# Two ordinary weight tiles per Strassen tile in a SwiGLU FFN, with the ordinary groups in three PSUM banks and the gated outputs held as one fp32 copy

## The chip, the cores and the metric

The kernel runs on one core of one Trainium2 chip. The core has a matrix engine (TensorE, "PE" in the profile, with its weight loads as "PEld"), a vector engine (VectorE, "DVE"), an activation engine (ScalarE, "ACT"), a general engine (GpSimd, "POOL") and a queue that issues the transfers from memory (SyncE, "SP"). Matrix products are collected in eight PSUM banks of 512 fp32 columns. The metric is the device time of one execution in microseconds (us), the median of a few runs. A lower time is better.

## The reference

Two layers work on 256 tokens of width 2048: a recurrent block and then sliding-window attention, each followed by a SwiGLU feed-forward network (FFN). The change concerns the FFN, which appears once in each layer:

```python
D_MODEL = 2048; SEQ = 256; D_FF = 5632

def swiglu_ffn(x, g, w_in, w_out):
    h = rms_norm(x, g)
    gate, up = jnp.split(h @ w_in, 2, axis=-1)
    return x + (jax.nn.silu(gate) * up) @ w_out
```

Everything is fp32. All weights are read once, so every product has 256 columns (the tokens) on one side.

## The kernel before

Weights arrive as tiles of 128 partitions x 1024 fp32 values (512 KB). A *tile* is one job of the list `self.jobs`. The loop `stream` (L309) takes the jobs in order: at job i it issues the load of job i+4 on SP's queue (`load`, L236), splits the weights of job i+3 (`split`, L281), and then emits the matmuls of job i. There are four buffers each for `raw`, `hi` and `lo`. A split makes from an fp32 tile a rounded high part (ACT, L295, or L287 for Strassen tiles) and the rest, the low part (DVE, L298, or L288). A product of two fp32 matrices is then three matmuls: high x high, high x low, low x high.

An **ordinary tile** (`group`, L378, and `products`, L327, whose matmuls are line L361) has two blocks of 128 input features (k) and four of 128 output features (f): 2 x 4 x 3 = 24 matmuls of 256 columns. Eight tiles make one *group* with four outputs of 128 x 256 (two gates and two ups). A group keeps its sums in PSUM banks in one of three ways. By default it takes four banks; where `sync` is given, two of its outputs then have the high x high product and the high x low product in two halves of one bank, and such a pair of matmuls can be issued as one of 512 columns ("h" in `PARTS`). With `paired` it takes two banks with two outputs in each and has no 512 wide matmuls. With `packed` it takes three: two outputs with a bank each, which can have 512 wide matmuls, and two outputs together in the third. The 512 wide matmuls come in runs of three, in the tiles that `sync` names (0, 2 and 5 of eight) and after a matmul of another kind (`pe_other`, L365, which sets `self.runs`).

A **Strassen tile** (`strassen`, L432, matmuls on L460) needs seven block products where an ordinary one has eight, so 21 matmuls. In exchange POOL adds and subtracts blocks of the weights (`sums`, L267, lines L277 to L279), and both ACT and DVE split three pieces: 768 columns of the tile and twice 512 columns of sums. The other side's sums (`form`, L477, POOL lines L488 to L491) are made once per FFN. A Strassen group is eight tiles too and takes four banks. The first `NS` = 4 groups of an FFN's first product are Strassen groups, the other 18 are ordinary.

`ffn` (L637) builds two lists, `turns` (32 Strassen tiles) and `ordinary` (144 tiles), and puts four ordinary tiles (`AHEAD`) first, then one Strassen tile and one ordinary tile in turn until the Strassen tiles are used up, and then the rest. Here this mixed stretch is called the Strassen stage. In it ordinary groups 4 to 8 are `paired`, so that 4 + 2 x 2 banks hold a Strassen group and two ordinary groups. The later ordinary groups take four banks with `sync`.

When an ordinary group ends, `done` (L687) pulls its four outputs out of PSUM (`pull`, L502: for an output with one half in use, a product with `rstd` on DVE; for one with two halves, a copy on ACT and an add on DVE ahead of it), and a background task applies SiLU (ACT), multiplies gate by up (DVE) and splits the result into a high and a low part (`split_act`, L520) which take one slot of 128 x 512 for each 128 x 256 output. When a Strassen group ends, `fast` (L643) combines the four banks with one ACT copy and four DVE adds into `U` and `V`; a task applies SiLU and the product (L134 on DVE), waits four ticks (`yield 4`; a tile has two ticks), has PE transpose the results (L369 and L372), and splits them from PSUM. Background tasks are issued when the planner's account of ACT and DVE time has room (`run_bg`, L208). Slots (58, `self.slots`) also hold the normalised input, the forms and the sums. The second product of the FFN, `ffn_out`, uses the split outputs `hid` and follows after all the tiles of the first.

Of the kernel before, what the change touches and what calls it, by code (L numbers as in the profile page):

```python
# [12 lines left out]
F32 = mybir.dt.float32  # L13
F32R = mybir.dt.float32r
AF = mybir.ActivationFunctionType
ALU = mybir.AluOpType
# [3 lines left out]
T = 256  # L20
DFF = 5632
ND = D // P
# [27 lines left out]
class Trunk:  # L50
# [17 lines left out]

    NS = 4
    AHEAD = 4  # L70
    SPACE = 14

    def __init__(self, ctx, tc, dram):
# [355 lines left out]
                    done([(p, two, st["bank"][b] if last_of else None) for p, two, b, last_of in st["ps"]])  # L429
            jobs.append((src(c), mm))  # L430

    def strassen(self, src, xs, forms, done, last):  # L432

        st = {}
        jobs = []
        for c in range(ND // 2):
            part = {}

            def mm(hi, lo, c=c, part=part):
                if c == 0:  # L440
                    st["ps"] = [self.bank() for _ in range(4)]
                    st["begun"] = set()
                ps = st["ps"]
                x2 = [self.need(xs[2 * c + kt]) for kt in range(2)]
                fh, fl = self.need(forms[c])
                A = lambda kt, b: tuple(x2[kt][:, q + b * P:q + b * P + P] for q in (0, T))
                S = lambda n: tuple(q[:, n * P:n * P + P] for q in (fh, fl))
                B = lambda n: tuple(q[:, n * T:n * T + T] for q in (hi, lo))
                s = part["set"]
                t1, t3, t2, t4 = (tuple(s[n + q][:, h * T:h * T + T] for q in (0, 1)) for n in (2, 4) for h in range(2))  # L450
                todo = [(0, 0, A(0, 0), B(1)), (1, 1, A(1, 0), B(3)), (1, 0, S(1), t2), (2, 0, S(0), t1),
                        (2, 1, S(2), t3), (3, 0, S(3), B(2)), (3, 1, A(1, 1), t4)]
                if self.other is not None:
                    self.runs = self.RUNS
                    self.other = None
                for n, (b, h, w, m) in enumerate(todo):
                    if n == 4:
                        self.half_tick()
                    for i, j in ((0, 0), (0, 1), (1, 0)):
                        self.nc.tensor.matmul(ps[b][:, h * T:h * T + T], w[i], m[j], start=b not in st["begun"],  # L460
                                              stop=c == ND // 2 - 1 and i == 1, skip_group_check=True)
                        st["begun"].add(b)
                        self.since += 1
                if last and c == ND // 2 - 1:
                    for q in self.sets:
                        for t in q:
                            self.free(t)
                    self.sets = None
                if last:
                    for q in (fh, fl):  # L470
                        self.free(q)
                if c == ND // 2 - 1:
                    done(ps)
            jobs.append((src(c), mm, part))
        return jobs

    def form(self, c, col, out):  # L477

        while len(self.slots) < self.SPACE:
            yield 1  # L480
# [156 lines left out]
    def ffn(self, l, xs, forms, r, gains, rn, out=None):  # L637
        hid = [Val() for _ in range(NH)]
        w = self.d[f"ffn_in{l}"]
        one = self.con[:, K_ID:K_ID + P]  # L640
        turns, ordinary = [], []
        for g in range(self.NS):
            def fast(ps, g=g):  # L643
                c1, U, V = self.t(), self.slot(F32), self.slot(F32)
                two = lambda q: q.rearrange("p (b t) -> p b t", b=2)
                twice = lambda q: q.unsqueeze(1).broadcast_to([P, 2, T])
                self.a(c1, ps[0][:, 0:T])
                self.tt(two(U[:, :]), two(ps[1][:, :]), twice(c1[:, :]), ALU.add)
                self.tt(two(V[:, :]), two(ps[2][:, :]), twice(U[:, 0:T]), ALU.add)
                self.tt(U[:, 0:T], ps[2][:, 0:T], V[:, T:2 * T], ALU.add)  # L650
                self.tt(V, ps[3], V, ALU.add)
                for b in ps:
                    self.free_bank(b)

                def task():
                    while not self.rv[r].ready:
                        yield 1
                    rs = [self.rstd[r][:, T + b:T + b + 1] for b in range(2)]
                    for q, s in ((U, 0), (V, 1)):
                        self.a(q[:, T:2 * T], q[:, T:2 * T], AF.Silu, scale=rs[s])  # L660
                    yield
                    for q, k, s in ((V, U, 0), (U, V, 1)):
                        self.stt(q[:, 0:T], q[:, 0:T], rs[s], k[:, T:2 * T], ALU.mult, ALU.mult)
                    yield 4
                    while not self.room():
                        yield 1
                    p = self.mbank()
                    for h in range(2):
                        for b, q in enumerate((V, U)):
                            self.pe_other(p[:, h * T + b * P:h * T + b * P + P], q[:, h * P:h * P + P], one,  # L670
                                          f=self.nc.tensor.transpose)
                    yield 1
                    self.free(U)
                    self.free(V)
                    for h in range(2):
                        while not self.slots:
                            yield 1
                        s = self.slot()
                        self.split_act(s, p[:, h * T:h * T + T])
                        hid[2 * g + h].ap = s  # L680
                        hid[2 * g + h].ready = True
                        yield
                    self.free_mbank(p)
                self.spawn(task())
            turns += self.strassen(lambda c, g=g: w[g, c], xs, forms, fast, g == self.NS - 1)
        for g in range(self.NS, NH // 2):
            def done(ps, g=g):  # L687
                rs = self.rstd[r][:, 0:T]
                early = not self.rv[r].ready
                v = [self.pull(p, r=None if early else rs) for p in ps]  # L690

                def task():
                    while not self.rv[r].ready:
                        yield 1
                    for h in range(2):
                        ga, up = v[2 * h], v[2 * h + 1]
                        if early:
                            self.tt(ga, ga, rs, ALU.mult)
                            self.tt(up, up, rs, ALU.mult)
                        self.a(ga, ga, AF.Silu)  # L700
                        yield
                        self.tt(ga, ga, up, ALU.mult)
                        while not self.slots:
                            yield 1
                        s = self.slot()
                        self.split_act(s, ga)
                        self.free_half(ga)
                        self.free_half(up)
                        hid[2 * g + h].ap = s
                        hid[2 * g + h].ready = True  # L710
                        yield
                self.spawn(task())
            self.group(lambda c, g=g: w[g, c], ND, xs, done, g == NH // 2 - 1, self.SYNC,
                       paired=2 * (g <= 2 * self.NS), jobs=ordinary)
        n = len(turns)
        self.jobs += ordinary[:self.AHEAD]
        for q in zip(turns, ordinary[self.AHEAD:]):
            self.jobs += q
        self.jobs += ordinary[self.AHEAD + n:]
        self.project(self.d[f"ffn_out{l}"], NH, hid, gains, rn, out)  # L720


# [610 lines left out]
```

## Time and profile before

| | us |
|---|---|
| median of 3 runs | 2023.13 (2022.03 to 2024.72) |
| the profiled execution | 2023.72 |
| its span, first to last instruction | 2021.9 |
| PE / DVE / ACT / POOL busy in the span | 1985.0 / 1412.9 / 1122.3 / 376.7 |
| mean granted PE clock | 0.995 |
| matmuls recorded | 16699 |

In the profile a line such as L361 is a line of the kernel above, and a group names the tile that is written, an arrow and the tiles that are read: `b` is a PSUM bank, `s` a slot, `raw`, `hi` and `lo` the weight buffers, `h` a 128 x 256 half, `x` the residual stream. "x848 | 115.6, 276 | 0.0" means 848 instructions, 115.6 us busy in total (overlaps counted once), 276 ns mean length of one, and the engine's idle time just before them. Matmuls are pipelined: each is listed with some 276 ns, though one starts about every 113 to 118 ns. The pace of PE is therefore read from starts, not from lengths.

### The profile page before, as it was taken

The page shows a single profiled execution, that of the slowest core. Times are in us where ns is not written, and L with a number is a line of the kernel's source. Part 1 is how long each engine was busy: PE and PEld are TensorE (multiplying, and loading weights), DVE is VectorE, ACT ScalarE, POOL GpSimd, SP SyncE. Part 2 cuts the span into 40 slices and gives each one's busy share as a digit, 9 for nine tenths or more (in the row PEclk, how much of TensorE's full clock was granted, in tenths as well). Part 3 has the DMA queues.
Part 4 walks back from the last instruction along what each step waited for, and adds up shares of the span by engine and source line. Part 5 has one row for each costly group of instructions (what it writes and reads, how often), then busy time and mean ns, then how long its engine had stood idle before and what let it go on. Part 6 is the DMA issues. An engine that isn't in the chain of part 4 may idle for free.

```text
span 2021.9 us, 41009 instructions
## 1 busy us (share of the span) xinstructions
PE 1985.0 (98%) x16699; PEld 1943.6 (96%) x16699; DVE 1412.9 (70%) x2089; ACT 1122.3 (56%) x1754; POOL 376.7 (19%) x356
## 2 busy tenths in 40 slices
PE   9999998999999999999999999989999999999999
PEld 9999998999999999999999889889999999999999
DVE  8988979999655655545667767889866556554553
ACT  6799766555444444434556776555555445444342
POOL 0000136774000000000002453576700000000000
PEclk9999999999999999999999999999999999999999
DMA  8555654555555555555555435455555655556663
GB/s 279 189 182 186 209 173 161 188 180 193 194 198 191 196 192 195 193 194 198 190 190 164 139 123 175 160 173 182 176 192 192 196 195 190 197 197 201 207 209 125
DMA packets 106204, 377.15 MB, mean 187 GB/s; under 512 B 11936, under 2 KB 14368, under 8 KB 106016
## 3 DMA queue, kind: packets, MB, share of 16 engines
q1 hardware_dynamic: 105408, 373.88, 56.0%
q8 instruction: 130, 2.13, 0.4%
q10 hardware_dynamic: 608, 0.66, 0.1%
q14 instruction: 58, 0.48, 0.1%
HBM read 371.88 MB, written 2.10 MB: 185 GB/s over the span
## 4 chain that ended last, share of the span: by engine, by line
PE 83%; DVE 7%; issue 3%; ACT 3%; POOL 2%; DMA 1%; ACTq 0%; DVEq 0%; POOLq 0%; SPq 0%
PE b L361 75%; PE b L460 4%; DVE lo L298 2%; DVE s L288 2%; PE b L372 1%; DVE s L130 1%; ACT hi L295 1%; ACT s L121 1%; DMA raw<-in_ffn_in 1%; DVE lo L288 1%; PE b L826 1%; POOL s L277 1%; PE b L369 1%; POOL s L489 1%; PE b L1012 1%
## 5 line engine op out<-in xcount | busy, mean ns | idle before, releaser
L361 PE MATMUL b<-s,hi 128*128 128x256 f32 (+1 forms) x9474 | 1309.1, 284 | 6.1 <-ACT hi L295 4.9
L361 PEld LDWEIGHTS b<-s,hi 128*128 128x128 f32 x9474 | 1207.5, 189 | 29.0 <-ACT hi L295 5.3
L298 DVE TENSOR_TENSOR lo<-raw,hi 128x1024 fp32r<-128x1024 f32 (+1 forms) x643 | 795.7, 1240 | 501.8 <-ACT hi L295 497.8
L295 ACT ACTIVATE hi<-raw 128x1024 fp32r<-128x1024 f32 (+1 forms) x643 | 675.8, 1054 | 623.4 <-PE b L361 562.1
L361 PE MATMUL b<-s,lo 128*128 128x256 f32 x4992 | 753.1, 277 | 0.0
L361 PEld LDWEIGHTS b<-s,lo 128*128 128x128 f32 x4992 | 655.1, 189 | 0.6
L277 POOL TENSOR_TENSOR s<-raw 128x512 f32<-128x512 f32 x64 | 121.4, 1896 | 115.0 <-DMA raw<-in_ffn_in 98.1
L288 DVE TENSOR_TENSOR s<-s,s 128x512 fp32r<-128x512 f32 x128 | 125.8, 985 | 17.5 <-ACT s L287 17.5
L1102 POOL TENSOR_TENSOR s<-s 128x128 f32<-128x128 f32 x32 | 14.7, 461 | 635.3 <-ACT s L121 630.7
L287 ACT ACTIVATE s<-s 128x512 fp32r<-128x512 f32 x128 | 79.7, 624 | 87.0 <-POOL s L277 48.1
L460 PE MATMUL b<-s,s 128*128 128x256 f32 x768 | 115.4, 283 | 4.4 <-DVE s L288 4.2
L460 PEld LDWEIGHTS b<-s,s 128*128 128x128 f32 x768 | 100.9, 189 | 6.3 <-DVE s L288 6.2
L460 PE MATMUL b<-hi,s 128*128 128x256 f32 x384 | 89.4, 282 | 1.1 <-DVE s L130 0.9
L288 DVE TENSOR_TENSOR lo<-raw,hi 128x768 fp32r<-128x768 f32 x64 | 80.4, 1256 | 0.4
L279 POOL TENSOR_TENSOR s<-raw,s 128x256 f32<-128x256 f32 x64 | 72.5, 1132 | 5.0
L489 POOL TENSOR_TENSOR s<-s 128x128 f32<-128x128 f32 x16 | 16.3, 1017 | 303.4 <-ACT s L121 303.4
L121 ACT ACTIVATE s<-s 128x256 f32<-128x256 f32 (+3 forms) x132 | 51.9, 439 | 37.4 <-POOL s L491 26.4
L460 PEld LDWEIGHTS b<-hi,s 128*128 128x128 f32 x384 | 68.4, 190 | 1.9 <-DVE s L130 1.9
L278 POOL TENSOR_TENSOR s<-raw,s 128x256 f32<-128x256 f32 x64 | 66.5, 1040 | 5.0
L460 PE MATMUL b<-lo,s 128*128 128x256 f32 x192 | 54.6, 284 | 7.6 <-DVE lo L288 7.6
L121 ACT ACTIVATE s<-x,par 128x256 fp32r<-128x256 f32 (+1 forms) x112 | 52.7, 497 | 16.4 <-DVE x L130 11.2
L130 DVE TENSOR_TENSOR s<-s,s 128x256 fp32r<-128x256 f32 (+3 forms) x100 | 46.1, 489 | 20.9 <-ACT s L121 20.9
(120 smaller groups left out, 1188.6 us busy)
## 6 DMA issues: line engine op xcount, KB each, us to landing
raw<-in_ffn_in SPq DMA_DIRECT2D x352, 512.0 KB, 3.4
raw<-in_ffn_out SPq DMA_DIRECT2D x176, 512.0 KB, 3.3
raw<-in_lru_in SPq DMA_DIRECT2D x62, 512.0 KB, 3.6
raw<-in_lru_out SPq DMA_DIRECT2D x32, 512.0 KB, 4.2
raw<-in_w_q SPq DMA_DIRECT2D x32, 512.0 KB, 3.4
raw<-in_w_o SPq DMA_DIRECT2D x32, 512.0 KB, 3.3
raw<-in_gate SPq DMA_DIRECT2D x8, 512.0 KB, 3.7
raw<-in_kv SPq DMA_DIRECT2D x8, 512.0 KB, 4.3
```

The costliest lines, as they stand in the source:

```text
L121: self.nc.scalar.activation(out, in_, func, **kw)
L130: self.nc.vector.tensor_tensor(out, a, b, op)
L277: tt(two(s[0][:, :]), b[:, 0:3:2, :], b[:, 1::-1, :], ALU.subtract)
L278: tt(s[1][:, 0:T], raw[:, 2 * T:3 * T], s[0][:, 0:T], ALU.subtract)
L279: tt(s[1][:, T:2 * T], raw[:, 3 * T:4 * T], s[1][:, 0:T], ALU.subtract)
L287: self.nc.scalar.activation(a, z, AF.Copy)
L288: self.nc.vector.tensor_tensor(b, z, a.bitcast(F32), ALU.subtract)
L295: high = self.ins(self.nc.scalar.activation(hi[:, q], raw[:, q], AF.Copy))
L298: self.nc.vector.tensor_tensor(lo[:, q], raw[:, q], hi[:, q].bitcast(F32), ALU.subtract)
L361: self.nc.tensor.matmul(*args, **kw)
L460: self.nc.tensor.matmul(ps[b][:, h * T:h * T + T], w[i], m[j], start=b not in st["begun"], stop=c == ND // 2 - 1 and i == 1, skip_group_ch ...
L489: tt(s[2], a11, a21, ALU.subtract)
```

## The change

1. **Order.** After the first four ordinary tiles, each Strassen tile is followed by two ordinary tiles (`OWN` = 2) instead of one, so the Strassen stage takes in 68 ordinary tiles instead of 36.
2. **Banks.** Ordinary groups 4 to 12 (those that have tiles in the stage) are `packed`: three banks, two outputs with 512 wide runs, in place of two banks without. Groups 13 and later are as they were.
3. **Outputs of the stage.** A counter `left` holds the number of Strassen tiles that are still to come. While it isn't zero, a finished ordinary group writes the products of gate and up into one fp32 slot (`both`), and a finished Strassen group copies its transposed results from PSUM into one fp32 slot. The new generator `later` waits until `left` is zero and then splits each half into its own slot and marks it ready.

```diff
+    OWN = 2
...
-    def strassen(self, src, xs, forms, done, last):
+    def strassen(self, src, xs, forms, done, last, left):
...
+                left[0] -= 1
...
+        left = [self.NS * ND // 2]
+
+        def later(g, s):
+            while left[0]:
+                yield 1
+            for h in range(2):
+                while len(self.slots) < 2:
+                    yield 1
+                q = self.slot()
+                self.split_act(q, s[:, h * T:h * T + T])
+                hid[2 * g + h].ap = q
+                hid[2 * g + h].ready = True
+                yield
+            self.free(s)
...
-                    for h in range(2):
-                        while not self.slots:
-                            yield 1
-                        s = self.slot()
-                        self.split_act(s, p[:, h * T:h * T + T])
-                        hid[2 * g + h].ap = s
-                        hid[2 * g + h].ready = True
-                        yield
+                    s = self.slot(F32)
+                    self.a(s, p)
                     self.free_mbank(p)
+                    yield
+                    yield from later(g, s)
...
+                    both = None
                     for h in range(2):
...
+                        if both is not None or h == 0 and left[0]:
+                            if h == 0:
+                                both = self.slot(F32)
+                            self.tt(both[:, h * T:h * T + T], ga, up, ALU.mult)
+                            self.free_half(ga)
+                            self.free_half(up)
+                            yield
+                            continue
...
+                    if both is not None:
+                        yield from later(g, both)
...
-                       paired=2 * (g <= 2 * self.NS), jobs=ordinary)
+                       packed=g <= (self.OWN + 1) * self.NS, jobs=ordinary)
         n = len(turns)
         self.jobs += ordinary[:self.AHEAD]
-        for q in zip(turns, ordinary[self.AHEAD:]):
-            self.jobs += q
-        self.jobs += ordinary[self.AHEAD + n:]
+        for i, q in enumerate(turns):
+            k = self.AHEAD + self.OWN * i
+            self.jobs += [q] + ordinary[k:k + self.OWN]
+        self.jobs += ordinary[self.AHEAD + self.OWN * n:]
```

More of the change, by code (lines that the diff above doesn't have):

```diff
@@ L674, in task @@
                     self.free(V)
[L675 to L682 removed]
+                    s = self.slot(F32)
+                    self.a(s, p)
                     self.free_mbank(p)
+                    yield
+                    yield from later(g, s)
                 self.spawn(task())
[L685 removed]
+            turns += self.strassen(lambda c, g=g: w[g, c], xs, forms, fast, g == self.NS - 1, left)
         for g in range(self.NS, NH // 2):
```

## The prediction

> **What bounds the kernel now.** I began with the page's first part, then set two stretches of equal length beside each other in the table of windows: from the first to the last Strassen tile of each FFN (32 Strassen tiles and, between them, 31 ordinary ones), and the stretch right behind it, ordinary tiles alone.
>
> ```profile
> PE 1985.0 (98%) x16699; PEld 1943.6 (96%) x16699; DVE 1412.9 (70%) x2089; ACT 1122.3 (56%) x1754; POOL 376.7 (19%) x356
> ```
> ```profile
> 304.20:494.10 189.90, 175.38 (x1437) 171.21 (x1436) 176.68 (x195) 106.69 (x166) 130.29 (x98) 0.99 0.53 177
> 494.10:684.00 189.90, 189.90 (x1597) 186.80 (x1596) 116.29 (x160) 92.22 (x124) 0.00 (x0) 1.00 0.60 195
> 1287.10:1481.30 194.20, 179.01 (x1436) 176.15 (x1435) 175.83 (x196) 108.19 (x167) 131.60 (x98) 0.96 0.54 176
> 1481.30:1675.50 194.20, 194.20 (x1631) 190.97 (x1630) 118.31 (x167) 95.46 (x127) 0.00 (x0) 1.00 0.60 193
> ```
>
> The columns are the stretch, then busy us (and instructions) of PE, PEld, DVE, ACT and POOL, the granted clock, the DMA share and GB/s. On the whole page PE is the bound. In the Strassen stages it isn't: PE misses 14.5 and 15.2 us, while DVE is busy 176.68 of 189.90 us (93%). Behind the stages DVE is busy 61% and PE always. The waits of PE in the two Strassen stretches (total, times, longest) say for whom:
>
> ```profile
> PE b L460 <- DVE lo L288: 5.5, 5, 1.6
> PE b L361 <- ACT hi L295: 4.7, 1, 4.7
> PE b L369 <- DVE s L134: 2.0, 3, 0.7
> ```
> ```profile
> PE b L369 <- DVE s L134: 9.5, 3, 3.8
> PE b L460 <- DVE s L288: 2.9, 4, 1.9
> ```
>
> Busy PE is not PE at its pace, so I read starts of matmuls from the timeline (start us, length, instruction, xcount, wait):
>
> ```profile
> 398.60 0.28 PE L460 MATMUL b<-hi,s 128*128 128x256 f32 x1
> ...
> 401.06 2.05 PE L361 MATMUL b<-s,hi 128*128 128x256 f32 x16
> 402.95 1.10 PE L361 MATMUL b<-s,lo 128*128 128x256 f32 x8
> 403.89 0.28 PE L460 MATMUL b<-hi,s 128*128 128x256 f32 x1
> ```
> ```profile
> 1346.07 0.47 PE L369 MATMUL b<-con,s 128*128 128x128 f32 x1 [3.83 <-DVE s L134]
> ...
> 1347.02 3.76 PE L361 MATMUL b<-s,hi 128*128 128x256 f32 x16
> 1350.58 1.51 PE L361 MATMUL b<-s,lo 128*128 128x256 f32 x8
> 1351.93 0.28 PE L460 MATMUL b<-hi,s 128*128 128x256 f32 x1
> ```
>
> An undisturbed Strassen tile takes 401.06 - 398.60 = 2.46 us (21 matmuls, 117 ns each), an ordinary one beside it 403.89 - 401.06 = 2.83 us (24, 118 ns). After a wait of 3.83 us the next ordinary tile takes 4.91 us: 2.08 us are lost to the clock besides the wait (the mean clock of that stage is 0.96). In the ordinary stage the groups of matmuls from 510 to 680 us are:
>
> ```profile
> L361 PE MATMUL b<-s,hi 128*128 128x256 f32 x848 | 115.6, 276 | 0.0
> L361 PE MATMUL b<-s,lo 128*128 128x256 f32 x502 | 76.4, 276 | 0.0
> L361 PE MATMUL b<-s,hi 128*128 128x512 f32 x75 | 21.2, 391 | 0.0
> ```
>
> 848 + 502 + 2 x 75 = 1500 runs of 256 columns in 170 us, 113.3 ns each, so 2.72 us a tile. There are two paces, and the 512 wide matmuls (the runs of three in `products`, L327) go with the quick one. A Strassen tile brings the slow one back.
>
> The sum for the stages: 32 x 2.46 + 31 x 2.83 + 1.4 us (16 transposes and 3 norm matmuls, an estimate at some 75 ns) = 167.8 us. The stretches take 189.9 and 194.2, so **22.1 + 26.4 = 48.5 us** are waits and the slow clock behind them. That is all the change can win apart from the pace.
>
> **Why DVE is late.** Its groups in the first Strassen stretch, one from the stretch behind (the last row), and single instructions from the timeline:
>
> ```profile
> L288 DVE TENSOR_TENSOR s<-s,s 128x512 fp32r<-128x512 f32 x63 | 63.9, 1016 | 6.4 <-ACT s L287 6.4
> L298 DVE TENSOR_TENSOR lo<-raw,hi 128x1024 fp32r<-128x1024 f32 x33 | 46.9, 1424 | 0.3
> L288 DVE TENSOR_TENSOR lo<-raw,hi 128x768 fp32r<-128x768 f32 x31 | 37.9, 1221 | 0.0
> ```
> ```profile
> L298 DVE TENSOR_TENSOR lo<-raw,hi 128x1024 fp32r<-128x1024 f32 x70 | 85.6, 1224 | 74.9 <-ACT hi L295 74.8
> ```
> ```profile
> 382.35 0.68 DVE L288 TENSOR_TENSOR s<-s,s 128x512 fp32r<-128x512 f32 x1
> 382.95 0.94 DVE L288 TENSOR_TENSOR lo<-raw,hi 128x768 fp32r<-128x768 f32 x1
> ```
> ```profile
> 1382.46 0.74 POOL L278 TENSOR_TENSOR s<-raw,s 128x256 f32<-128x256 f32 x1
> ...
> 1395.47 1.28 POOL L277 TENSOR_TENSOR s<-raw 128x512 f32<-128x512 f32 x1 [1.69 <-DMA raw<-in_ffn_in]
> ```
>
> A Strassen tile costs DVE 2 x 1.02 + 1.22 = 3.25 us, an ordinary one 1.42: 4.67 of the pair's 5.29 us of PE. The rest of DVE's 176.7 us (148.7 are these rows) is 28.0 us of evacuation, SwiGLU and norm, 0.88 a pair: 5.55 us against 5.29. DVE cannot hold the pair's pace; that is the bound.
>
> **The change part by part.** *Two ordinary tiles per Strassen tile* (`OWN`, the loop at L717): the same work in another order. PE's round is 2.46 + 2 x 2.83 = 8.12 us; DVE's is 3.25 + 2 x 1.42 = 6.09, plus background. This is the 28 us as before, plus four more ordinary groups that now end in the stage (about 4 us each: eight steps of the 0.35 us that a pull takes below, and room for POOL), some 44/32 = 1.4: 7.5 us, 92%. Per tile it falls further, because POOL's sums come once in 8.1 us rather than in 5.3 and the same L298 takes 1224 ns without POOL beside it. So DVE gains at least 0.6 us a round where it lost 0.3, and the three tiles of lead that `hi`/`lo` allow can fill. Each step moved brings its DMA, splits and sums along; SP's queue issues one 512 KB load a tile in the new order, at the 177 to 195 GB/s of both stretches, and POOL's sums are needed later than now. I take the DVE waits as gone but for 1 us a layer.
>
> The bound here is the share of DVE and POOL that can't overlap. The Trainium skill, SBUF — State Buffer, Who interferes with whom, says that a DVE instruction with two SBUF inputs contends with a GpSimd instruction that reads SBUF, and that the loser fully blocks. The longer rows beside POOL agree; a pair that was wholly serial would need more than the trace shows, as the second rival works out from rows.
>
> *The wait at the first stage's start* (4.7 us, and with the slow tile behind it 6.4): ACT stood behind the form of the last operand.
>
> ```profile
> 315.15 0.63 ACT L121 ACTIVATE s<-s 128x512 fp32r<-128x512 f32 x1 [4.20 <-POOL s L491]
> ```
>
> POOL had a tile's sums between the two forms. With a tile more between sums they come later, but the forms stay. It can be 0 to 6.4 us; I leave 2, and 1 us in layer 1.
>
> *Transposes of a Strassen group* (`fast`, L643; `yield 4`, L664). The transposes stand in PE's queue a fixed number of tiles behind the group, and the chain of four DVE adds and two products has to be done by then:
>
> ```profile
> 1386.15 2.05 PE L361 MATMUL b<-s,hi 128*128 128x256 f32 x16
> ```
> ```profile
> 1387.94 0.68 DVE L130 TENSOR_TENSOR s<-b,t 128x512 f32<-128x512 f32 x1
> ...
> 1393.11 1.35 DVE L134 SCALAR_TENSOR_TENSOR s<-s,rstd,s 128x256 f32<-128x256 f32 x2
> ```
>
> The group's last matmul came just before the ordinary tile at 1386.15; the products ended at 1394.5, 8.3 us later, with three splits between the adds. Four ticks are two tiles, 5.3 us as they stand and 5.7 with two ordinary ones, and by the planner's own budget of DVE time the products are issued half a tile to a tile later than now. So it shrinks from 9.5 us (and 3 x 2.1 of clock) to, I take, 3 us in layer 1 and 0.5 in layer 0; bounds 0 and all 15.8.
>
> *Three banks per ordinary group* (`packed`, L378). Four Strassen banks and three leave one free, where two pairs of banks took turns: a new group's first bank is now one that was just evacuated. This adds a wait, eight group starts a layer; queued behind it on PE is everything. Each start lies behind a Strassen tile (2.46 us of cover), and the last tile of a group works its outputs one by one, so evacuation begins early:
>
> ```profile
> 385.52 1.41 DVE L130 TENSOR_TENSOR h<-b,rstd 128x256 f32<-128x256 f32 x4
> ```
> ```profile
> 386.13 0.28 PE L460 MATMUL b<-hi,s 128*128 128x256 f32 x1
> ```
>
> The four outputs of an ordinary group were pulled from 385.52 to 386.93, while its last tile ended at 386.13. Wide outputs add two copies on ACT and two adds of some 0.35 us, a quarter of that row. Price 0 to 2.4 us a start; I take 0.2, the row's nearest, 1.6 a layer. The Trainium skill, Perfetto Trace Analysis, Optimizing Tensor Performance, asks that independent groups rotate through different banks so that evacuation overlaps the next group; by that rule this part speaks against the change, as the third rival does.
>
> *512 wide runs.* Sync steps 0, 2 and 5 of eight bring runs. Half of tile 0 and tiles 4, 6 and 7 stay slow behind a Strassen tile: 3.5 of 8 at 0.11 us. 62 ordinary tiles in the stage give 27 slow ones where 31 were: -0.4 us a layer, and -0.2 for those behind the stage, about -1 in all. Without the runs it would be +3.4 a layer.
>
> *One fp32 copy* (`later`): a Strassen group gets one more ACT copy, of 512 columns, and both kinds split 24 halves after the stage, at 0.35 to 0.45 us a step about 10 us of DVE and of ACT. Under PE's 190 us there, with DVE 61% busy, this costs nothing; if the cover fails, 1 us, which I take for both layers. The copy occupies one slot instead of two.
>
> The sum: -48.5 + (2 + 1 + 0.5 + 1.6) + (1 + 1 + 3 + 1.6) + 1 - 1 = **-36.8 us**. The profiled execution took 2023.7 (its span 2021.9 and 1.8 around it), the median is 2023.1: 2023.1 - 36.8 = **1986 us**, 1976 to 1996 as its own range.
>
> **The rivals.** (1) *The waits hang on the order of issue, not on DVE's load*: transposes and the first tiles wait as before, half of the 48.5 remains: 2023.1 - 24 + 4 = about 2003 us. For: the transposes' place is counted in tiles, and layer 1, where they wait longest, has DVE less busy (175.83 of 194.2 us, 91%) than layer 0 (93%). Against: in layer 0 most waits are for splits.
>
> (2) *DVE and POOL stay the bound.* If they never overlapped, a round would take DVE 2 x 0.68 + 0.94 + 2 x 1.22 = 4.74, POOL 1.28 + 2 x 0.74 = 2.76 and 0.88 of background, 8.4 us against 8.1. The stage would be 11 us longer than PE's, a layer: 2023.1 - 48.5 - 1 + 22 + 2 = about 1998. Against: the pair would by this have taken 3.52 + 2.76 + 0.88 = 7.2 us, and took 189.9/32 = 5.9.
>
> (3) *The bank handover*: PE waits for the evacuation of wide banks at each of 16 starts. It undoes the gain from 2.3 us more a start; at 4 us, with 2 us of slow clock after each, it is 16 x 6 - 48 = +48: 2070 us, slower. For: one spare bank, and a chain of ACT copy, add and product behind a split of 1.42 us. Against: the early pull above.
>
> (4) It moves nothing: the waits reappear in the ordinary stage, where 24 splits come at once. DVE's 61% there speaks against it.
>
> **How the numbers follow.** Forecast 0.64, (1) 0.12, (2) 0.12, (4) 0.04, (3) 0.08. A measurement of this kernel can tell about 0.2% (4 us) from no change. Faster 0.88, same 0.04, slower 0.08. The range goes from 1974.6 (every wait gone and the pace gained: 2023.1 - 49.5, with 1 us for the splits) to 2007 (the first rival, and 4 us).
>
> **What would show it.** Right: in the windows of the stage PE near 100% and the clock near 1.0, DVE near 80 to 90%; waits on L288 below 2 us a layer; the stage from first to last Strassen tile some 257 us. The transposes' wait below 3 us in layer 1; ordinary groups starting without a wait on L130; 512 wide matmuls inside the stage and stretches at 113 ns. Wrong: DVE at 95% or more in the longer stage; L361 waiting on the evacuation every 21 us; a busy POOL that makes the three splits of a Strassen tile as long as now.

## The result, and the profile after

The changed kernel took 2113.25 us (median of 3 runs, 2111.33 to 2117.97) where the one before took 2023.13: the ratio is 1.0449, with an interval of 1.042 to 1.0479. It is 90 us slower, and the forecast was 37 us faster. The lines of the changed kernel that are named here lie one further down than before: the ordinary matmuls are L362, the Strassen ones L461, the splits L296 and L299 (ordinary, ACT and DVE) and L288 and L289 (Strassen), POOL's sums L278 to L280, and the evacuation on DVE is L131.

The first part of the page, and the first line of its fourth part (the chain that ended last), of the changed kernel:

```profile
PE 2017.2 (96%) x16555; PEld 1965.6 (93%) x16555; DVE 1354.4 (64%) x2109; ACT 1131.1 (54%) x1782; POOL 328.0 (16%) x356
...
PE 58%; POOL 7%; DMA 7%; DVE 5%; ACT 5%; issue 3%; POOLq 0%; ACTq 0%; DVEq 0%; SPq 0%
```

and that first line of the fourth part for the kernel before:

```profile
PE 83%; DVE 7%; issue 3%; ACT 3%; POOL 2%; DMA 1%; ACTq 0%; DVEq 0%; POOLq 0%; SPq 0%
```

DVE became less busy (70% to 64%), and yet PE's share of the chain fell. The two lines can't be compared as they stand: the chain of the changed kernel, followed back, breaks off at 319.8 us, so its shares add up to 85%. Of the part that it covers, PE has 68%. What took PE's place is clearest in the chain of the first Strassen stage alone, by line (first the changed kernel from 324 us to the end of the stage, then the kernel before; the view ends its lines at a fixed width):

```profile
by line: DMA raw<-in_ffn_in 22.8%; PE b L362 19.2%; DVE lo L299 10.6%; POOL s L278 9.8%; ACT hi L296 7.7%; POOL s L280 7.3%; issue 6.8%; POOL s L279 5.3%; PE b L461 3.8%; DVE h L131 1.4%; ACT s L288 1.1%; DVE s L131 0.9%; ACT hi L288 0.8%;
```
```profile
by line: PE b L361 20.3%; PE b L460 16.6%; issue 12.0%; DVE s L288 10.9%; DVE lo L298 9.2%; DVE lo L288 6.5%; DVE s L130 6.0%; DVE h L130 2.4%; POOL s L277 2.1%; ACT hi L295 1.8%; DMA raw<-in_ffn_in 1.8%; DVE s L134 1.4%; PE b L372 1.1%; PO
```

Summed by engine, DVE's share of the stage fell from 38% to 15%, while DMA's rose from 2% to 23%, POOL's from 6% to 22% and ACT's from 4% to 10%. So not one engine but four stations hold the chain. That is the mark of a latency that runs through several engines, none of which is full.

The table of windows, for the two Strassen stages (first to last Strassen tile) and for the stretch of ordinary tiles behind the first (columns as before: PE, PEld, DVE, ACT, POOL, clock, DMA share, GB/s):

```profile
302.74:624.52 321.78, 276.97 (x2087) 267.81 (x2086) 200.71 (x274) 151.96 (x232) 110.38 (x101) 0.93 0.46 157
1333.38:1655.06 321.68, 279.54 (x2087) 269.89 (x2086) 196.41 (x273) 152.53 (x232) 107.58 (x101) 0.93 0.47 158
```
```profile
624.52:814.42 189.90, 189.90 (x1586) 186.41 (x1585) 114.30 (x158) 91.58 (x123) 0.00 (x0) 1.00 0.58 192
```

The two stages take 321.8 and 321.7 us where the prediction had some 257: 2 x 65 = 130 us, which is all of the difference between 2113 and 1986. Behind the stage nothing is lost. In it DVE is busy 62%, ACT 47%, POOL 34%, and even the DMA moves less per second than behind it.

PE's waits in the first stage and in the second:

```profile
PE b L362 <- DVE h L131: 37.5, 8, 5.9
PE b L362 <- ACT hi L296: 3.6, 1, 3.6
PE b L373 <- DVE s L135: 1.1, 3, 0.4
```
```profile
PE b L362 <- DVE h L131: 30.7, 8, 4.9
PE b L362 <- ACT hi L296: 4.1, 2, 3.6
PE b L370 <- DVE s L135: 3.7, 3, 1.5
```

The first row of each is the 16 starts of ordinary groups, and the wait is the one that the third rival named: the new group's bank has not been evacuated. Taken by itself this view says that the three banks are at fault. The chain says otherwise. It is shown here for one round of Strassen tile and two ordinary tiles, up to one of those group starts (start us, us, what; the short "issue" pieces are left out):

```profile
441.58 3.17 DMA raw<-in_ffn_in
...
444.89 1.29 POOL s L278
...
446.25 0.75 POOL s L279
...
447.06 1.08 POOL s L280
...
448.70 1.05 ACT hi L296
...
449.78 1.23 DVE lo L299
451.00 0.67 DVE h L131 x2
...
451.72 4.39 PE b L362 x20
```

The evacuation (h, 0.67 us) is short, and it stands at the end of a chain that began with a load ten microseconds earlier. And the chain closes on itself: with that DVE lo ended at 451.00, the next load can start. Where no group starts, the chain runs from the low part straight into that load, with nothing of PE between, as in a later round:

```profile
481.01 1.24 DVE lo L299
...
482.26 3.21 DMA raw<-in_ffn_in
```

POOL's first sums show the tours (start us, us, instruction, idle before and for whom):

```profile
435.40 1.30 POOL L278 TENSOR_TENSOR s<-raw 128x512 f32<-128x512 f32 x1 [6.43 <-DMA raw<-in_ffn_in]
...
444.88 1.28 POOL L278 TENSOR_TENSOR s<-raw 128x512 f32<-128x512 f32 x1 [6.20 <-DMA raw<-in_ffn_in]
...
454.35 1.34 POOL L278 TENSOR_TENSOR s<-raw 128x512 f32<-128x512 f32 x1 [6.21 <-DMA raw<-in_ffn_in]
```

A tour takes 9.48 and 9.47 us in these quick rounds, and 10.1 on average over the stage's 31 (POOL's first sum at 293.0, the last one's at 607.5). PE's round is 8.12. Three rounds out of four PE runs on what was split ahead, and at the next start of a group it pays for all of them.

**Why the loop closes.** ACT's queue in the same round:

```profile
440.94 1.04 ACT L296 ACTIVATE hi<-raw 128x1024 fp32r<-128x1024 f32 x1
446.20 0.63 ACT L288 ACTIVATE s<-s 128x512 fp32r<-128x512 f32 x1 [4.22 <-POOL s L278]
448.17 0.63 ACT L288 ACTIVATE s<-s 128x512 fp32r<-128x512 f32 x1 [1.34 <-POOL s L280]
448.70 1.04 ACT L296 ACTIVATE hi<-raw 128x1024 fp32r<-128x1024 f32 x1
449.65 0.64 ACT L122 ACTIVATE t<-b 128x256 f32<-128x256 f32 x2
450.18 0.84 ACT L288 ACTIVATE hi<-raw 128x768 fp32r<-128x768 f32 x1
```

Two things meet. First, the built program's order is not that of the lines: the two splits of the sums of a Strassen tile (446.20, 448.17) stand on ACT *ahead of* the split of the ordinary tile before it (448.70) and of the ended group's evacuation (449.65). ACT idles 4.22 + 1.34 us for POOL, and everything behind waits too. Second, there are four raw buffers, and the load of a job goes into the buffer of the job four before it. With one ordinary tile between (S O S O), a Strassen tile takes the buffer of the Strassen tile two rounds back. With two between (S O O S O O), the Strassen tile before it is three jobs back, so the fourth is the ordinary tile just ahead of that. So the load of Strassen tile k+1 waits for the split of the ordinary tile before Strassen tile k; that split stands on ACT behind the sum splits of Strassen tile k; those wait for POOL; POOL waits for the load of Strassen tile k. That is one tour of load, sums, sum split and ordinary split per round. In a quick round PE has no part in it. Behind a group start it has: from 451.72 the chain stays on PE until 459.07, when the next split on ACT can start.

### The profile page after: what moved, and what is told of

It is laid out like the page before. It is cut to its first block, busy times and chain, and to the rows that moved or that the text cites. A ratio compares the mean times of both kernels' runs of the same rounds, so it can differ in the third digit from the quotient of the medians.

```text
span 2111.5 us, 40705 instructions
## 1 busy us (share of the span) xinstructions
PE 2017.2 (96%) x16555; PEld 1965.6 (93%) x16555; DVE 1354.4 (64%) x2109; ACT 1131.1 (54%) x1782; POOL 328.0 (16%) x356
## 4 chain that ended last, share of the span: by engine, by line
PE 58%; POOL 7%; DMA 7%; DVE 5%; ACT 5%; issue 3%; POOLq 0%; ACTq 0%; DVEq 0%; SPq 0%
PE b L362 54%; DMA raw<-in_ffn_in 7%; DVE lo L299 3%; POOL s L278 3%; ACT hi L296 3%; POOL s L280 2%; POOL s L279 2%; PE b L461 1%; PE b L373 1%; ACT s L122 1%; PE b L1037 1%; PE b L370 1%; DVE h L131 0%; ACT s L288 0%; DVE s L131 0%
## 5 line engine op out<-in xcount | busy, mean ns | idle before, releaser
L362 PE MATMUL b<-s,hi 128*128 128x256 f32 (+1 forms) x9321 | 1342.1, 289 | 77.1 <-DVE h L131 68.8
L362 PEld LDWEIGHTS b<-s,hi 128*128 128x128 f32 x9321 | 1223.7, 191 | 112.6 <-DVE h L131 71.9
L299 DVE TENSOR_TENSOR lo<-raw,hi 128x1024 fp32r<-128x1024 f32 (+1 forms) x643 | 791.6, 1233 | 447.7 <-ACT hi L296 445.4
L296 ACT ACTIVATE hi<-raw 128x1024 fp32r<-128x1024 f32 (+1 forms) x643 | 675.1, 1052 | 537.4 <-PE b L362 483.7
L362 PE MATMUL b<-s,lo 128*128 128x256 f32 x4992 | 765.0, 280 | 3.4 <-DVE lo L299 3.2
L362 PEld LDWEIGHTS b<-s,lo 128*128 128x128 f32 x4992 | 665.2, 191 | 5.5 <-DVE lo L299 4.8
L288 ACT ACTIVATE s<-s 128x512 fp32r<-128x512 f32 x128 | 80.9, 632 | 305.1 <-POOL s L278 218.1
L289 DVE TENSOR_TENSOR s<-s,s 128x512 fp32r<-128x512 f32 x128 | 93.8, 734 | 216.9 <-ACT s L288 216.8
L278 POOL TENSOR_TENSOR s<-raw 128x512 f32<-128x512 f32 x64 | 90.9, 1420 | 410.2 <-DMA raw<-in_ffn_in 372.2
L461 PE MATMUL b<-s,s 128*128 128x256 f32 x768 | 112.3, 281 | 0.0
L461 PEld LDWEIGHTS b<-s,s 128*128 128x128 f32 x768 | 99.9, 189 | 0.0
L461 PE MATMUL b<-hi,s 128*128 128x256 f32 x384 | 88.8, 281 | 0.0
L122 ACT ACTIVATE s<-s 128x256 fp32r<-128x256 f32 (+3 forms) x180 | 69.8, 429 | 31.7 <-POOL s L493 20.4
L131 DVE TENSOR_TENSOR s<-s,s 128x256 fp32r<-128x256 f32 (+3 forms) x148 | 63.6, 455 | 20.7 <-ACT s L122 20.7
L280 POOL TENSOR_TENSOR s<-raw,s 128x256 f32<-128x256 f32 x64 | 68.6, 1073 | 4.9
L461 PEld LDWEIGHTS b<-hi,s 128*128 128x128 f32 x384 | 68.4, 190 | 0.0
L289 DVE TENSOR_TENSOR lo<-raw,hi 128x768 fp32r<-128x768 f32 x64 | 60.8, 949 | 0.7 <-ACT hi L288 0.7
L461 PE MATMUL b<-lo,s 128*128 128x256 f32 x192 | 54.0, 281 | 0.9 <-DVE lo L289 0.9
L279 POOL TENSOR_TENSOR s<-raw,s 128x256 f32<-128x256 f32 x64 | 54.0, 844 | 5.0
```

The costliest lines, as they stand in the source:

```text
L122: self.nc.scalar.activation(out, in_, func, **kw)
L131: self.nc.vector.tensor_tensor(out, a, b, op)
L278: tt(two(s[0][:, :]), b[:, 0:3:2, :], b[:, 1::-1, :], ALU.subtract)
L279: tt(s[1][:, 0:T], raw[:, 2 * T:3 * T], s[0][:, 0:T], ALU.subtract)
L280: tt(s[1][:, T:2 * T], raw[:, 3 * T:4 * T], s[1][:, 0:T], ALU.subtract)
L288: self.nc.scalar.activation(a, z, AF.Copy)
```

## The experiments

Two theories came first. **A** is the third rival: the handover of banks is the cause. **B**: PE meets late splits there, and the handover only sets where they are met. Each kernel was timed beside the kernel before (2022 to 2024 us).

**Two banks in place of three, all else as changed.** The edit:

```diff
-                       packed=g <= (self.OWN + 1) * self.NS, jobs=ordinary)
+                       paired=2 * (g <= (self.OWN + 1) * self.NS), jobs=ordinary)
```

> The changed kernel, but with the stage's ordinary groups back in two banks with two outputs each (no 512 wide runs in the stage). Theory A (the loss is the bank handover: a new ordinary group waits for banks that are being evacuated, 68.8 us of waits on h L131 and some 2 us of slow clock behind each of 16): these waits vanish, and 2113 falls by 69 + 16 x 2.2 = 104 us or more, to 1985 to 2010, faster than before. Theory B (the order of two ordinary tiles per Strassen tile is itself the loss: the chain of DMA, sums and splits becomes late): it stays above 2050, and other waits take the place of those on h L131.

Measured: 2101.67 us, ratio 1.0391 (1.0376 to 1.0407). Of the 90 us lost, the three banks account for 12. PE's waits over the whole of this kernel:

```profile
PE b L362 <- ACT hi L296: 33.0, 31, 1.6
PE b L370 <- DVE s L135: 15.7, 6, 3.3
PE b L373 <- DVE s L135: 12.5, 6, 2.6
PE b L461 <- DVE lo L289: 10.6, 11, 2.7
```

The waits on h are gone, and nearly as many others stand in their place, spread over splits and transposes. A fell.

**One ordinary tile per Strassen tile, with the banks and copies of the change** (`OWN = 1`):

> The changed kernel, but with one ordinary tile per Strassen tile as before; three banks and the fp32 copy stay. Theory A: the handover costs here too, at the four or five group starts of each stage, 4 to 7 us each with the slow clock: 2023 + 32 to 70 = 2055 to 2090. Theory B: about 2023, because the order is the old one.

Measured: 2030.65 us, 1.0038 (1.0025 to 1.0051). The handover does cost something by itself, 8 us, but far less than was expected here.

**One ordinary tile, two banks: the fp32 copy alone:**

> Of the change only the fp32 copies of the stage's outputs and their later splits stay; order and banks are those of before. Both theories: within 4 us of the kernel before (2019 to 2027). If it is slower by more, the copies carry part of the loss.

Measured: 2021.48 us, 0.9995 (0.9985 to 1.0004). The copy costs nothing that shows.

**As changed, but the evacuation copies are issued ahead of the next splits:**

```diff
+        with self.tc.issue_after(self.evac[0]), self.tc.issue_after(self.evac[1]):
+            self.split_of(i)
```

> The changed kernel with one thing more: in the queues of ACT and DVE the splits of the tile four ahead stand behind the evacuation of a group that has just ended (in the changed kernel two splits of Strassen sums stand ahead of the evacuation's two copies on ACT, and wait for POOL's sums and these for a DMA). Theory A1 (the handover is long because the evacuation stands in line behind these splits): waits on h L131 fall from 68.8 to below 20 us, the time to 2000 to 2040. Theory A2 (the evacuation of two wide outputs, copy on ACT and adds on DVE, is itself too long for one spare bank): the waits stay above 50 us and the time above 2085.

Measured: 2062.68 us, 1.0196 (1.0179 to 1.0213). PE's waits on the evacuation fell from 68.8 to 3.7 us; splits and transposes took over (16.4 us for ACT hi, 17.8 for a transpose). The waits are as theory A1 had them, the time lies between the two theories. Half of the loss went with an order of issue. The loop was left in most rounds, but not in all: six of the 31 tours of each stage take only 4.3 to 6.5 us. In one of them (sums at 438.8 and 444.7) the ordinary split, at 435.81, stands ahead of the sum splits on ACT.

Here **Theory L** (the loop above) was formed. It says that either of two edits opens the loop: put the splits in the order of the tiles, or add a raw buffer.

**Splits in order.** With both numbers of banks; the edit makes the splits of a tile follow those of the tile before, on ACT and DVE:

```diff
+            with ExitStack() as st:
+                for e in self.last:
+                    st.enter_context(self.tc.issue_after(e))
...
+            self.last = (c, e)
...
+        self.last = (high, low)
```

> Two banks per ordinary group as in the first experiment, and the splits of each tile stand behind those of the tile before it in the queues of ACT and DVE (so far the splits of a Strassen tile's sums stood ahead of the split of the ordinary tile before it). Theory L (a loop of latencies sets the round of three tiles: split of the ordinary tile, DMA into its raw buffer 3.3 us, POOL's sums 3.3, split of the sums, and behind it on ACT the split of the next ordinary tile: 9.4 to 10 us a round where PE needs 8.1): the loop is open, waits of PE on splits (57 us in the first experiment) fall below 20, the time to 1985 to 2015. Theory M (ACT, DVE and POOL have too much work or stand in each other's way in this order): above 2060.

> The changed kernel (three banks) with the splits in the order of the tiles, and nothing else. Theory L: what the evacuation and the splits stand behind comes earlier, so waits on h L131 fall from 68.8 to 10 to 35 us, and the time from 2113 to 2000 to 2045. Theory M: above 2080.

Measured: 1992.16 us with two banks, 0.9845 (0.983 to 0.986), and 1995.63 with three, 0.9862 (0.9847 to 0.9876). The second is the changed kernel with nothing but this order: 2113 became 1996, a little below what was expected. Its ACT queue (here L301 is the split of an ordinary tile and L292 those of a Strassen tile):

```profile
445.62 1.06 ACT L301 ACTIVATE hi<-raw 128x1024 fp32r<-128x1024 f32 x1 [2.06 <-issue]
446.59 0.62 ACT L292 ACTIVATE s<-s 128x512 fp32r<-128x512 f32 x1
448.70 0.63 ACT L292 ACTIVATE s<-s 128x512 fp32r<-128x512 f32 x1 [1.50 <-POOL s L281]
449.24 0.83 ACT L292 ACTIVATE hi<-raw 128x768 fp32r<-128x768 f32 x1
450.46 1.06 ACT L301 ACTIVATE hi<-raw 128x1024 fp32r<-128x1024 f32 x1 [0.38 <-PE b L467]
```

The ordinary split (445.62) now stands ahead of the sum splits, so its buffer comes free before POOL is waited for. PE's waits on h are 4.6 us in all, with the same three banks.

With both orders, of the splits and of the evacuation, and three banks:

> The changed kernel (three banks) with the splits in the order of the tiles and the evacuation ahead of the next tile's splits. Theory L: both waits go, 1985 to 2020, below the kernel with the evacuation first alone (2063) by 40 us or more. Theory M: within 15 us of 2063.

Measured: 1996.39 us, 0.9861 (0.9846 to 0.9876). Once the loop is open, the evacuation's place gives nothing.

**A fifth raw buffer, in the old order** (two banks, loads five jobs ahead, two slots fewer):

```diff
-    LD = 4
+    LD = 5
...
-        self.slots = deque(range(58))
+        self.slots = deque(range(56))
...
-        raw, src = self.raw[i % 4], self.jobs[i][0]
+        raw, src = self.raw[i % 5], self.jobs[i][0]
```

> Two banks as in the first experiment, the old order of splits, but a fifth raw buffer and loads five tiles ahead (two slots fewer). Theory L: a Strassen tile's load no longer waits for the split of the ordinary tile four ahead in the same loop, so the time falls from 2102 by 50 us or more, to 1985 to 2045. Theory M: a buffer gives no work back, 2085 to 2105.

Measured: 1999.09 us, 0.988 (0.9863 to 0.9896), 102.6 us below the same kernel with four. The Trainium skill, Perfetto Trace Analysis, Identifying Performance Opportunities, says that consistent bubbles can mean too few buffers for the next tile to be allocated. This run agrees (102.6 us for one buffer); the runs with the splits in order add that with the same four buffers an order of issue does as much.

**Order and buffer together**, and **the kernel before with its splits in order**:

> Two ordinary tiles, two banks, splits in the order of the tiles, and a fifth raw buffer with loads five ahead. Theory L: the loop is open already by the order, so the buffer adds nothing: 1985 to 1998, within 6 us of the kernel with order alone (1992). If part of the loop is left there, 1975 to 1985.

> The kernel before (one ordinary tile per Strassen tile, two banks, no fp32 copies) with the splits in the order of the tiles. If the 48 us of waits of its Strassen stages come from DVE's load, as the prediction had it, order gives nothing: 2010 to 2030. If they come from the order of splits, as with two tiles, they go: 1975 to 2000.

Measured: 1987.27 us, 0.9822 (0.9807 to 0.9836), the fastest version found; and 2021.33, 0.9993 (0.9984 to 1.0003). In the kernel before the order gives nothing. There the loop is not what binds: in the chain of its first stage, shown above, loads have 2% and DVE 38%, as the prediction had it. A fifth buffer was not tried there. The stages of the fastest version:

```profile
303.70:560.98 257.28, 256.79 (x2180) 256.33 (x2179) 219.21 (x258) 147.90 (x213) 113.77 (x96) 1.00 0.59 195
1269.94:1529.21 259.27, 256.86 (x2180) 256.20 (x2179) 222.84 (x258) 148.34 (x213) 113.16 (x96) 1.00 0.59 195
```

257.3 and 259.3 us, PE waits for almost nothing, DVE is busy 85%: what the prediction had asked for.

**Three ordinary tiles per Strassen tile** (`OWN = 3`, PE's round 10.95 us): in the old order with four buffers, with five (57 slots), and in order with four.

> Three ordinary tiles per Strassen tile, two banks, the old order of splits and four raw buffers. Theory L: a Strassen tile's raw buffer is then that of the Strassen tile before, and PE needs 2.46 + 3 x 2.83 = 10.95 us a round where the loop takes 9.4 to 10.5; so PE hardly waits on splits (below 20 us, 57 in the first experiment): 1985 to 2015. If it is only the order of splits that costs, whatever the round, it stays above 2060.

> Three ordinary tiles per Strassen tile with a fifth raw buffer and loads five ahead (one slot fewer), the old order of splits. In the run with three and four buffers the loads came in bunches of three and took 5.4 us instead of 3.3, so the loop was about 12 us against PE's 10.95, and it was slow though I had put the loop at 9.4 to 10.5. Theory L with that length: the fifth buffer takes the Strassen tile's load out of the loop, so PE's waits on splits (42 us) fall below 15 and the time from 2078 to 1990 to 2020. If the order of splits costs by itself, whatever the buffers, it stays above 2050.

> Three ordinary tiles per Strassen tile, two banks, four raw buffers, and the splits in the order of the tiles. Theory L (the loop closes only because a Strassen tile's sum splits stand ahead of an ordinary tile's split on ACT): open, waits on splits below 15 us, 1985 to 2010. If the round of three ordinary tiles is slow for a cause of its own: above 2040.

Measured: 2077.79 us, 1.0272 (1.0255 to 1.029); 2083.92, 1.0298 (1.0281 to 1.0315); and 1990.82, 0.9842 (0.9828 to 0.9857). The first two were misses, and fell where the other reading (the order costs by itself, whatever the buffers) had put them: a longer round does not outrun the loop, because the loop grows with it. How it grows is read from the traces, after the results; no run tests it by itself. With four buffers, from the chain:

```profile
484.43 5.43 DMA raw<-in_ffn_in
...
490.00 1.28 POOL s L278
```

The load takes 5.43 us in place of 3.2. It is the second of three that are issued within two microseconds (at 483.52, 484.43 and 485.52, and landed after 5.07, 5.43 and 5.59). In the changed kernel loads come in threes too (at 441.58, 442.49 and 443.58), but there the Strassen tile's is the first of them: it landed after 3.17 us, the two behind it after 4.95 and 5.07. With five buffers and a round of four, a Strassen tile again takes the buffer of the ordinary tile just ahead of the Strassen tile before: the same relation as four buffers in a round of three. In its queue on ACT two ordinary splits stand behind the sum splits, and the tour takes 11.8 us (from the load at 477.32 to the end of the low part that frees the next buffer, at 489.09), more than 10.95. In order (the third), neither matters. The tours, on average over the first stage, agree: 12.4 and 12.5 us in the first two, and 10.9 in order, which is PE's round. What the expectations had left out is that the number of buffers counts only against the length of the round.

**The loop's length, directly.** POOL's first sum is done twice, with the same values, in the kernel with two banks: in the old order, in order, and in order with five buffers.

```diff
         tt(two(s[0][:, :]), b[:, 0:3:2, :], b[:, 1::-1, :], ALU.subtract)
+        tt(two(s[0][:, :]), b[:, 0:3:2, :], b[:, 1::-1, :], ALU.subtract)
```

> The first experiment (two banks, old order of splits, 2102 us) with POOL's first sum of each Strassen tile done twice, the same values, about 1.36 us more in the loop. Theory L: each of 64 rounds becomes longer by that: 2102 + 60 to 87, so 2160 to 2190. If POOL's latency is not in a loop: 2095 to 2125.

> The same doubled sum in the kernel with the splits in the order of the tiles (1992 us). Theory L: the loop is open and the longer sum is hidden, 1992 to 2010. If the order only shifted a cost of POOL's work or of its contention with DVE: 2030 or more.

> Two banks, splits in order, five raw buffers, and POOL's first sum done twice (the same values). Theory L (latency through the weight buffers): the fifth buffer lets the load of a Strassen tile be issued a tile (2.8 us) earlier, so the sum's 1.3 us more should find room: 1987 to 2010 us, waits on splits under 15 us in both stages together. Rival (POOL's extra reading of SBUF slows DVE and ACT, whatever the buffers): about as far above the version without the doubled sum as with four buffers, some 60 us, so 2035 to 2060 us.

Measured: 2184.33 us, 1.0799 (1.0783 to 1.0815); 2055.5, 1.0165 (1.0148 to 1.0182); and 2013.77, 0.9962 (0.9947 to 0.9976). In the old order the 64 doubled sums cost 2184.3 - 2101.7 = 82.7 us, 1.29 us each, one to one with the 1.28 us of the instruction: all of POOL's time is on the path, though POOL is busy a third of the stage. The average tour of the first stage shows the same: 10.1 us with two banks and 11.4 with the doubled sum, against 8.2 in order and 8.3 with the fifth buffer alone, where PE's round is 8.12.

In order the doubled sums cost 63.3 us (2055.5 - 1992.2), which Theory L had not expected and the rival had (2030 or more). The fifth buffer brings it to 26.5 us (2013.8 - 1987.3), between what the two theories expected and 4 us above Theory L's: so 37 of the 63 us were room in the buffers. A likely reading is that the wait for POOL is off the ordinary split but the tour is still there over two rounds; this was not shown. Where the other 26.5 come from, 0.4 us a Strassen tile, was not separated. A candidate is that POOL's sums and DVE's splits shut each other out, as in these rows of the last kernel (L305 is the low part of an ordinary tile, L279 and L280 the sum and its repetition):

```profile
459.95 2.35 DVE L305 TENSOR_TENSOR lo<-raw,hi 128x1024 fp32r<-128x1024 f32 x2
```
```profile
461.23 2.23 POOL s L279
...
463.53 1.30 POOL s L280
```

The sum that began at 461.23, while DVE's second split ran on to 462.30, ended at 463.46, 1.16 us behind it: it takes 2.23 us in place of 1.28. That is not the doubling's doing, for the first sums without it are as long wherever a split is under way. But 1.28 us more of POOL in a round can take as much from DVE, which is 85% busy without it.

## Why the prediction was wrong

*DVE's load bounds the kernel before, 48.5 us of waits hang on it, and two ordinary tiles give them back.* Right as a mechanism, once the loop is open. The changed kernel with nothing but its splits in order takes 1995.63 us, 28 of the forecast 37 us below the kernel before. That the fastest version's 1987.27 us stand so near the forecast of 1986 is in part luck, for it leaves out the three banks and has a buffer more. The kernel before in order (0.9993) excludes that those waits came from the order of the splits. The other half of the first rival, the transposes' place, has no run of its own; with that place unchanged their wait is gone in the fastest version. In the changed kernel DVE's own load is no longer the bound either (62%).

*"SP's queue issues one 512 KB load a tile in the new order ... and POOL's sums are needed later than now."* This is the step that failed, and with it the term that rests on it, waits of 1 us a layer in the stage. It counted loads and sums as work, by rate: one load a tile, 2.76 us of POOL in a round of 8.12. It never asked what each load waits for. A load needs its raw buffer, and the buffer's last reader changed with the round: from a Strassen tile two rounds back to an ordinary tile of the round before. All of the terms for the tour were in rows of the kernel before (POOL 1.28 + 2 x 0.74, ACT's splits 0.63 and 1.04, DVE's 1.22), or one query of the transfers away (3.2 us from issue to landing). Added up, they give 8.9 us, above 8.12 even without the gaps between them, and the tours measured 9.47 when quick and 10.1 on average. 31 tours, 2.0 us each above PE's round, are 63 us a layer, nearly all of the 65. In PE's own time these are 45 us of waits in the first stage (the three rows above and three below 1 us) and some 20 us of slow pace: PE is busy 276.97 us there and 256.79 in the fastest version. At 451.72 the first eight matmuls after a wait of 4.46 us start in 1.87 us, 234 ns each where 118 are usual, and the mean clock of the stage is 0.93.

*Three banks.* Priced at 1.6 us a layer, 3.2 in all. With the splits in order it measures 1995.63 - 1992.16 = 3.5 us, with the loss of the quick pace in it. In the old order it is 11.6 us, and 8 us with one ordinary tile. The third rival had the sign, the place and nearly the size of the wait (4 us, then 2 of clock; 68.2 us over 16 starts are 4.3), and not the cause: with two banks the kernel is still 79 us slower than before.

*512 wide runs.* Priced at -1 us. No run has them apart from the three banks; with these they make the 3.5 us. In the stage they bring little of the quick pace that the price counted on. A place in the changed kernel without it:

```profile
454.45 1.31 PE L362 MATMUL b<-s,hi 128*128 128x512 f32 x5
...
456.06 1.10 PE L362 MATMUL b<-s,hi 128*128 128x256 f32 x8
457.01 1.10 PE L362 MATMUL b<-s,lo 128*128 128x256 f32 x8
457.95 1.10 PE L362 MATMUL b<-s,hi 128*128 128x256 f32 x8
458.89 0.29 PE L461 MATMUL b<-hi,s 128*128 128x256 f32 x1
```

After the wide matmuls the next 24 take 458.89 - 456.06 = 2.83 us, 118 ns each: the slow pace, ahead of the next Strassen tile. Over the first stage, 116 of 1302 matmuls of 256 columns in ordinary tiles are followed by the next start within 115.5 ns, and 268 of 1302 with the splits in order; in the fastest version, which has no wide ones, 1 of 1488.

*The fp32 copy*, 1 us: it costs nothing that shows (0.9995 by itself). *Transposes*, 0.5 and 3 us: near (0.8 + 1.1 and 3.7 + 1.2 us), and in the fastest version PE's wait for those products no longer appears.

*The second rival.* By its own terms, 8.38 us against 8.12, its stage is 8 us longer than PE's and not 11, and its time some 1992 us. Its objection doesn't hold either: the rows above show the splits and the sums shut out from each other, and of the 7.2 us that were set against 5.9, the 0.88 of background isn't all of that kind. The rival missed the cause all the same, for DVE is busy 62% of the changed stage.

Of the signs named in the prediction, "L361 waiting on the evacuation" came true, every 40 us or so rather than every 21.

## What to carry to other kernels

When the order of jobs changes, work out for each buffer of a ring who its previous owner is, and add up the latency from that owner's release to the next one; if the sum is above the round, no engine has to be full for the stage to be late. When many engines have like shares of the chain and none of them is above two thirds busy, look for such a loop, and don't take the line that PE waits for as the cause: here it was where the queue ended, and removing it moved the wait. Before a buffer is added, look at the order within each engine's queue: a wait for a slow producer put ahead of ready work cost 118 us here (2113.25 - 1995.63), and a few lines that pin the order took it away.

## What the runs showed of the hardware

Loads of 512 KB that were issued alone took 3.2 us to land (3.19, 3.26 and 3.22 for those at 451.03, 453.93 and 456.80 of the changed kernel). Of three that are issued within two microseconds, the later two took 4.95 to 5.59 in the places given above, and the first 3.17 or 5.07.

The low part of a split on DVE (which reads two tiles, `raw` and `hi`) and a sum on POOL did not run side by side. In the fastest version all 22 first sums that began while such a low part ran ended 1.15 to 1.17 us behind its end, and all 17 low parts of 128 x 1024 that began while one sum ran and met no other ended 1.08 us behind that sum's end. By themselves the first sum takes 1.28 us and such a low part 1.22.

And 512 wide matmuls do not always bring the quick pace of 113 ns: inside the Strassen stage they were mostly followed by matmuls at 118 ns, with the condition for it still open.
